# A Toeplitz block moved to VectorE, one load and one projection handed out earlier, in the convolution and scan stage of a hybrid encoder

## The chip, the cores and the metric

One NeuronCore of a Trainium2 chip runs the whole kernel. The metric is the device time of one execution in microseconds; lower is better. Engine names are those of the profile: PE is TensorE (PEld its weight loads), DVE is VectorE, ACT is ScalarE, POOL is GpSimd, SP is SyncE, whose queue here issues almost all DMAs.

## What is computed

The reference is a two-layer encoder on 512 positions and 1024 features. The change lies in the mixer of layer 0:

```python
z = h @ w_in                      # 1024 -> 512 (za) + 512 (zg) + 512 (u)
ya = conformer_conv(za, zg, ...)  # a = za * sigmoid(zg); depthwise conv of 31 taps
                                  # + conv_b; layer norm over channels; silu
yb = s5_mixer(u, ...)             # 32 groups of 16 channels, 64 complex states, two
                                  # directions; gelu; gated by sigmoid(y @ glu_w + glu_b)
x  = x + concat([ya, yb]) @ w_out
```

After it come a SwiGLU feed-forward, a layer of neighbourhood attention and a second feed-forward, which the change leaves alone.

## The kernel before, in words

**Scan.** The state-space branch is cut into chunks of 8 positions. Eight pieces of 4 groups go through the loop at lines 880 to 901. For piece `i`, PE makes the chunk inputs `v` (`piece_v`), ACT copies them to `vt`, and DVE runs the scan over chunks (`g_scan`, line 832: two multiplies, two scan instructions, a multiply and the sums into `S2`). In the same pass DVE prepares tables for piece `i+2` (`g_turn`) and `i+4` (`make_pb`), and PE transposes and multiplies pieces `i+2` (`piece_t`, `piece_k`). `piece_k` fills `kf`, the blocks of the response inside a chunk.

**Projections.** The matmuls for `zg` and `za` are a generator, `proj_all` (lines 723 to 752), which `heavy(n)` advances by n units. A unit is one 128x512 f32 matmul, which the trace shows as two records. There are 64: 32 for `zg`, then 32 for `za`. Each group of 8 takes one weight chunk from `W`. Of the last 8 units of `za`, every second one is followed by a DVE multiply at line 743, which gates one quarter of `an`. The loop calls `heavy(HV[0])` and `heavy(HV[1])`, with `HV = (3, 4)`: 7 units a pass, 56 in all. `heavy(100)` at line 928, after the loop, hands out the other 8. So on DVE the four gating multiplies stand behind the scan of piece 7.

**Weights.** While `W.hold` is set, `W.ahead()` after each chunk issues a load on SP into one of three `wraw` buffers. The load called at the last `za` chunk reuses the buffer of that same chunk, so it waits on SP until the last `za` matmul. After `heavy(100)`, loads come from `split()`, which also makes a high part (`whi`, ACT, line 89) and a low part (`wlo`, DVE, line 91).

**kd and T.** After the loop, four SP DMAs (lines 923 to 925) write `kf` to a DRAM buffer `kd`, and a POOL DMA (line 926) adds one more block to it. `T` (2 MB, lines 988 to 992) is read back from `kd` in the Toeplitz order. These three SP loads are issued after the convolution.

**Convolution.** `to_chunks(an, AC)` transposes the gated `an` on PE and copies it on ACT to `AC` (line 794). The convolution (lines 966 to 986) multiplies `AC` by Toeplitz blocks `tc`. They are made in pairs by `make_tc(n)`: 16 ACT instructions (line 765), each with one column of a mask as scale. There are three slots for pairs: two in `tca` and one in `tcb`. Pairs 0 and 2 are made in the scan loop, the others in the convolution: 4 ahead of it, and 6, 8, 10, 12, 14 after blocks 1, 3, 5, 7, 9. After every 4 blocks DVE adds `conv_b` (tile `cbB`, loaded by SP at line 954) and sums for the layer norm (lines 983 and 985).

**Order of DVE.** The tables `Q` for the scan's output (16 half tables of three DVE instructions each, `g_q`) are handed out by a planner, `bgV`. Each `tick(ns)` adds credit, each instruction takes its estimated cost from it, and `charge` takes credit for other DVE work. `W.ahead()` after block 7 puts two splits there (line 981).

**Output.** `out_y(i, hq)` multiplies `U` by `T` and `S2` by `Q`; `ln_mean()` follows the first `out_y` on PE, and DVE's subtraction at line 1053 follows it. `ln_scale()` with the matmul at line 1062 stands in the middle of the third `out_y`.

**Memory.** The pool `ep` ends at line 930, and the pool `lp` takes its place from the same address on: first `AC` (8704 bytes a partition), then four `Q` of 8192 bytes. `AC` so covers `vecs`, `work` and the scan's `vt`; `kf`, which lies 35424 bytes into `ep`, is covered by the last `Q`. A tile waits for the last use of what it covers.

```python
 22  HV = (3, 4)
882          heavy(HV[0])
888          heavy(HV[1])
891          run(g_scan(i))
926      PL.dma_start(out=kd_ap(7, 1), in_=kfr[0:16, 1], accum_op=ALU.add)
928      heavy(100)
977              if n % 2 and n + 5 < 16:
978                  make_tc(n + 5)
```

Of the kernel before, what the change touches and what calls it, by code (L numbers as in the profile page):

```python
# [9 lines left out]
F32 = mybir.dt.float32  # L10
# [3 lines left out]
ALU = mybir.AluOpType  # L14
# [4 lines left out]
QKV_ORDER = (0, 2, 1, 3, 4, 5)  # L19

CAP = 3000.0
HV = (3, 4)
QN, QT = 0, 2
LN, LT, LV = 1, 4, 6
LNA, MAH = (1, 3, 5), (0, 1, 2)
# [4 lines left out]
P = 128  # L30
# [4 lines left out]
G = 32  # L35
NCH = 64
LCH = 8
TAPS = 31
NLAG = 40
# [75 lines left out]
def tile_hybrid_encoder(ctx, tc, x, mix_norm, ffn_norm, ffn_w_gate, ffn_w_up, ffn_w_down,  # L115
# [4 lines left out]
    nc = tc.nc  # L120
    V, A, PE, PL = nc.vector, nc.scalar, nc.tensor, nc.gpsimd
# [41 lines left out]
    xp = ctx.enter_context(tc.tile_pool(name="xp", bufs=1))  # L163
# [17 lines left out]
    def xtile(name, dt=F32):  # L181

        i = xslot[0] % 10
        xslot[0] += 1
        if i < 8:
            return xp.tile([P, 512], dt, tag=f"x{i}", name=name)
        if i == 8:
            xpair_[:] = [xp.tile([P, 2, 512], dt, tag="x8", name=name)]
        return xpair_[0][:, i - 8]
# [83 lines left out]
    class Background:  # L273
# [20 lines left out]
        def tick(self, ns):  # L294
            self.credit = min(self.credit, CAP) + ns * self.share
            while self.credit > 0 and (self.jobs or self.fill):
                if self.jobs:
                    self.step()
                else:
                    self.step_fill()  # L300
# [31 lines left out]
    def pt(shape, name, pool=None, dt=F32):  # L332
        return (pool or mp).tile(shape, dt, tag=name, name=name)
# [78 lines left out]
    mask16 = pt([P, 16], "mask16")  # L412
# [24 lines left out]
    def tt(o, a, b, op):  # L437
        V.tensor_tensor(out=o, in0=a, in1=b, op=op)
        return cost(o.free_size())
# [180 lines left out]
    for k in range(KD):  # L620
        t = xtile("xT")
# [14 lines left out]
    def make_cb(i):  # L636
        cb = CB[i % 2]
        for d in range(2):
            h = slice(64 * d, 64 * d + 64)
            A.activation(out=cb[h, :, :, d], in_=CT[h, :, 4 * i:4 * i + 4], func=AF.Copy)  # L640
# [17 lines left out]
    for i in range(4):  # L658
# [7 lines left out]
        for kk in range(2):  # L666
            k = 2 * i + kk
            for j in range(4):
                c = slice(j * P, (j + 1) * P)
# [7 lines left out]
        if i == 1:  # L677
# [6 lines left out]
            for t in range(4):  # L684
# [4 lines left out]
                         in_=ps[:, 64:64 + 4 * TAPS].rearrange("p (t j) -> p t j", t=4), func=AF.Copy)  # L689
# [3 lines left out]
            for t in range(LCH):  # L693
                p0 = 64 * (t % 2) + 16 * (t // 2)
                nc.sync.dma_start(out=wv[p0:p0 + 16],
                                  in_=bass.AP(tensor=wdb.tensor, offset=wdb.offset + t,
                                              ap=[[WPAD, 16], [16 * WPAD, G], [1, NLAG]]))
            A.activation(out=hgb, in_=col[:, R_GB:R_GB + 4], func=AF.Copy, scale=0.5)
        if i == 2:
            for r in range(2):  # L700
                ps = psb("ct")
                for t in range(4):
                    PE.transpose(out=ps[:, t * P:(t + 1) * P],
                                 in_=cnat[r][:, t].rearrange("p d n -> p (d n)"), identity=ident)
# [50 lines left out]
    slots = [tca[:, 0], tca[:, 1]]  # L755
    wvs = wv.rearrange("p (h s) l -> p h s l", h=2)
    tcs = {}

    def g_tc(n):

        t = slots[n // 2 % 3]
        for i in range(2):
            tcs[n + i] = t[:, :, i]
        for c in range(16):
            A.activation(out=t[:, :, :, c], in_=wvs[:, :, n:n + 2], func=AF.Copy, scale=mask16[:, c:c + 1])
            yield 1

    def make_tc(n):
        for _ in g_tc(n):
            pass  # L770

    def g_tc_early():
        yield from g_tc(0)
# [2 lines left out]
    def heavy(n):  # L776
        for _ in range(n):
            if next(proj_all, 0) == 0:
                return
# [3 lines left out]
    def to_chunks(src, dst):  # L783

        tick(2000)
        for b in range(4):
            for t2 in range(2):
                h = slice(64 * t2, 64 * t2 + 64)
                ps = psb("U")
                for g in range(8):  # L790
                    PE.transpose(out=ps[0:64, g * 64:g * 64 + 64],
                                 in_=src[h, b * 8 + g].rearrange("p j c -> p (j c)"),
                                 identity=ident[h, h])
                A.activation(out=dst[h, b * 8:b * 8 + 8], in_=ps[0:64].rearrange("p (g k) -> p g k", g=8),
                             func=AF.Copy)
# [60 lines left out]
    def piece_v(i):  # L856

        g0 = 4 * i
        pp = ppb[:, i % 2]
        pv = psb("v")  # L860
        for q in range(2):
            for g in range(4):
                for c in range(0, P, VW):
                    PE.matmul(out=pv[c:c + VW, (q * 4 + g) * 64:(q * 4 + g + 1) * 64], lhsT=pp[:, q, g, c:c + VW],
                              rhs=U[:, g0 + g] if c == 0 else U[:, g0 + g, ::-1], start=True, stop=True)
        v = ep.tile([P, 2, 256], F32, tag="vt", name="vt", bufs=2)
        A.activation(out=v, in_=pv.rearrange("p (q n) -> p q n", q=2), func=AF.Copy)
        vin[i] = v
# [11 lines left out]
    for i in range(NPC):  # L880
        piece_v(i)
        heavy(HV[0])
        if i + 2 < NPC:
            piece_t(i + 2)
            piece_k(i + 2)
        if i + 4 < NPC:
            make_cb(i + 4)
        heavy(HV[1])
        if i + 1 < NPC:
# [12 lines left out]
    for h in range(2):  # L902
# [4 lines left out]
                     in1=dmask.unsqueeze(1).to_broadcast([P, G, 16]), op=ALU.mult)  # L907
# [7 lines left out]
    def kd_ap(slot0, nj, pairs=1, run=512):  # L915

        base = kd[:, :, :]
        return bass.AP(tensor=base.tensor, offset=base.offset + slot0 // 2 * 16 * 1024 + slot0 % 2 * 512,
                       ap=[[1024, 16 * nj]] + ([[16 * 1024, pairs]] if pairs > 1 else []) + [[1, run]])
# [4 lines left out]
    nc.sync.dma_start(out=kd_ap(8, 4), in_=kfr[64:128, 1])  # L924
    nc.sync.dma_start(out=kd_ap(9, 3), in_=kfr[16:64, 1])
    PL.dma_start(out=kd_ap(7, 1), in_=kfr[0:16, 1], accum_op=ALU.add)

    heavy(100)
    W.hold = False
    early.close()  # L930
    lp = mixp.enter_context(tc.tile_pool(name="lp", bufs=1))
    AC = pt([P, G, NCH + 4], "AC", lp)
    PL.memset(AC[:, :, 0:2], 0.0)
    PL.memset(AC[:, :, NCH + 2:NCH + 4], 0.0)

    Q = {i: lp.tile([P, 2, 8, 8, 16], F32, tag="Q", name="Q", bufs=4) for i in (0, 2, 1, 3)}

    def g_q(i, hf):
        g0 = 8 * i + 4 * hf
# [5 lines left out]
        for o, a, b, op in ((0, cr, ci, ALU.add), (1, ci, cr, ALU.subtract)):  # L945
            yield tt(w[0], wr, a, ALU.mult)
            yield tt(w[1], wi, b, ALU.mult)
            yield tt(Q[i][:, o, 4 * hf:4 * hf + 4], w[0], w[1], op)


    cbB = tmp([P, 16, 16], "rstdB", 1)
    for h in range(2):
        src = conv_b[0, 256 * h:256 * h + 256]
        nc.sync.dma_start(out=cbB[64 * h:64 * h + 64],
                          in_=bass.AP(tensor=src.tensor, offset=src.offset, ap=[[0, 64], [1, 256]]))
# [5 lines left out]
    tick(1000)  # L961
    to_chunks(an, AC[:, :, 2:NCH + 2])
    make_tc(4)
    yc = pt([P, LCH, 16, 16], "an")
    lns = tmp([P, 4, LCH], "lns", 1)
    for b in range(4):
        ps = psa("conv")
        for gi in range(4):
            n = 4 * b + gi
            t = tcs.pop(n)  # L970
            for h in range(2):
                for l in range(5):
                    PE.matmul(out=ps[64 * h:64 * h + 64, gi * P:gi * P + P],
                              lhsT=AC[:, 16 * h + n, l:l + NCH],
                              rhs=t[:, h, :, 8 * l:8 * l + 8],
                              start=(l == 0), stop=(l == 4))
            if n % 2 and n + 5 < 16:
                make_tc(n + 5)
            tick(2200)
        if b == 1:  # L980
            W.ahead()
        gs = slice(4 * b, 4 * b + 4)
        V.tensor_tensor(out=yc[:, :, gs], in0=ps.rearrange("p (g c t) -> p t g c", g=4, t=LCH),
                        in1=cbB[:, gs].unsqueeze(1).to_broadcast([P, LCH, 4, 16]), op=ALU.add)
        V.tensor_reduce(out=lns[:, b], in_=yc[:, :, gs].rearrange("p t g c -> p t (g c)"), axis=AX.X, op=ALU.add)
        bgV.charge(1200)

    T = xp.tile([P, LCH, G, 16], F32, tag="xgl", name="T")
    T2 = T.rearrange("p (m o) g c -> p m o (g c)", o=2)
    nc.sync.dma_start(out=T[0:64].rearrange("p (m o) g c -> p m (o g c)", o=2), in_=kd_ap(0, 4, 4, 1024))  # L990
    for o in range(2):
        nc.sync.dma_start(out=T2[64:128, :, o], in_=kd_ap(1 + o, 4, 4))

    yn = xp.tile([P, LCH, 16, 16], F32, tag="xgh", name="yn")

    def out_y(i, hq, between=None):
# [4 lines left out]
        for gi in range(4):  # L1001
            if gi == 2 and between is not None:
                between()
            for h in range(2):
                g = h * 16 + i * 8 + hq * 4 + gi
                o = ps[64 * h:64 * h + 64, gi * P:(gi + 1) * P]
                q8 = Q[g // 8]
                PE.matmul(out=o, lhsT=U[:, g], rhs=T[:, :, g], start=True, stop=False)
                for r in range(2):
# [6 lines left out]
    GC = 0.7978845608028654  # L1016
    yg = pt([P, 4, S], "AC", lp)

# [59 lines left out]
    def mix_tile(n):  # L1078
        return lp.tile([P, 4, S], F32R, tag="Q", name=n, bufs=4)

# [47 lines left out]
    for p2 in range(2):  # L1128
        wh, wl = W.next()
        W.ahead()  # L1130
        for mi in range(2):
            m = 2 * p2 + mi
            ps = psb("glu")
            for k in (0, 2, 1, 3):
                c = slice(mi * P, mi * P + P)
# [60 lines left out]
    for m in range(KD):  # L1196
        ps = psa("dn")
        for a, b in ((0, 8), (8, 16), (16, 22)):
            wh, wl = W.next()
            W.ahead()  # L1200
            for k in range(a, b):
                mm3(ps, wh[:, k - a], wl[:, k - a], gh[:, k], gl[:, k], k == 0, k == NF - 1)
        t = xtile("x2")
        V.tensor_tensor(out=t.rearrange("p (c t r) -> p t r c", **dims),
                        in0=ps.rearrange("p (t r c) -> p t r c", **dims),
                        in1=x1[m].rearrange("p (t r c) -> p t r c", **dims), op=ALU.add)
# [37 lines left out]
    def ring(name, dt=F32):  # L1244
        return ap_.tile([P, S], dt, tag="ring", name=name, bufs=6)
# [122 lines left out]
    for n, cg in enumerate(QKV_ORDER):  # L1368
# [46 lines left out]
        else:  # L1415
            ssh = tmp([P, 4, 8], "ssh")
            qs = []
            for j in range(4):
                t = ring("qs")
# [58 lines left out]
    for h in range(2):  # L1478
        for j in range(4):
# [4 lines left out]
            t = fp.tile([P, 512], F32, tag="xn3", name="xn3", bufs=4)  # L1484
# [3 lines left out]
        for i in range(NF // 2):  # L1488
# [5 lines left out]
            for kk, j in steps:  # L1494
                k = 2 * i + kk
                c = slice(j * P, (j + 1) * P)
# [4 lines left out]
        for j in range(4):  # L1501
            t = xn3[h, j]
# [30 lines left out]
```

## Time and profile before

| what | value |
|---|---|
| median of 3 runs | 1257.42 us (1256.78 to 1258.33) |
| profiled execution, its own time | 1258.42 us |
| span of its instructions | 1256.5 us |
| PE busy | 1213.6 us (97%) |
| DVE busy | 674.1 us (54%) |
| ACT busy | 470.1 us (37%) |
| POOL busy | 37.1 us (3%) |

The profile shows one execution. Its own time exceeds its span by 1.9 us, which lie around the instructions, and it lies 1.0 us above the median of the runs. Positions in the trace are us from the start of the span. In a timeline a row gives start, length, engine, line, operation, tile written and tiles read, count, and in brackets how long the engine was idle before and what ended that.

### The profile page before, as it was taken

The numbers are of one execution on the slowest core, as the hardware profiler recorded it, in microseconds if no ns is written. First come the engines' busy times: TensorE is split into PE (matmuls) and PEld (weight loads), VectorE is DVE, ScalarE is ACT, GpSimd is POOL, SyncE is SP. The second block draws the span as 40 slices with busy tenths as digits, with TensorE's granted clock in tenths as the row PEclk, the third lists the DMA queues.
The fourth block names the chain that finished last, engine by engine and source line by source line (L and its number), as shares of the span: only waits on it lengthen the run. The fifth ranks groups of instructions, "written<-read, shape, count | busy, mean of one in ns | idle before, by whom it ended". The sixth has DMA issues, their size and how long they took to land.

```text
span 1256.5 us, 16175 instructions
## 1 busy us (share of the span) xinstructions
PE 1213.6 (97%) x6427; PEld 961.7 (77%) x6427; DVE 674.1 (54%) x1163; ACT 470.1 (37%) x837; POOL 37.1 (3%) x90
## 2 busy tenths in 40 slices
PE   7999758999999999999999999999999999999998
PEld 3554557888888888888888887668888888888886
DVE  7999965764444444333337554655544444442322
ACT  4544575543333232222225455544333323231120
POOL 1000000000000000000000002320000000000000
PEclk9999898999999999999999999999999999999999
DMA  7411130333333333333343543212333333333321
GB/s 155 92 51 51 55 86 17 109 93 101 101 94 92 100 90 91 105 96 93 97 155 126 151 136 106 66 39 85 100 101 93 92 100 89 96 101 101 118 101 33
DMA packets 173154, 118.04 MB, mean 94 GB/s; under 512 B 21193, under 2 KB 153593, under 8 KB 173080
## 3 DMA queue, kind: packets, MB, share of 16 engines
q1 hardware_dynamic: 172616, 115.92, 31.9%
q10 hardware_dynamic: 400, 1.07, 0.4%
q8 instruction: 50, 0.82, 0.3%
q14 instruction: 24, 0.20, 0.1%
q0 software_dynamic: 64, 0.03, 0.0%
HBM read 109.04 MB, written 7.96 MB: 93 GB/s over the span
## 4 chain that ended last, share of the span: by engine, by line
PE 84%; ACT 3%; DMA 1%; DVE 1%; issue 0%; SPq 0%; POOL 0%; ACTq 0%; DVEq 0%; POOLq 0%
PE up L199 6%; PE gate L199 6%; PE gate L201 6%; PE up L201 6%; PE gate L200 6%; PE up L200 6%; PE qkv L1398 3%; PE qkv L1400 3%; PE qkv L1399 3%; PE dn L200 3%; PE dn L199 3%; PE dn L201 3%; PE dn L1499 3%; PE dn L1497 3%; PE dn L1498 3%; PE o L1360 3%
## 5 line engine op out<-in xcount | busy, mean ns | idle before, releaser
L91 DVE TENSOR_TENSOR wlo<-wraw,whi 128x1024 fp32r<-128x1024 f32 x176 | 212.9, 1213 | 265.7 <-ACT whi L89 264.4
L89 ACT ACTIVATE whi<-wraw 128x1024 fp32r<-128x1024 f32 x176 | 183.4, 1044 | 283.3 <-issue 113.9
L199 PE MATMUL gate<-xgh,whi 128*128 128x512 f32 x352 | 137.2, 390 | 0.0
L199 PE MATMUL up<-xgh,whi 128*128 128x512 f32 x352 | 137.1, 390 | 0.0
L201 PE MATMUL gate<-xgh,wlo 128*128 128x512 f32 x352 | 137.0, 389 | 0.0
L201 PE MATMUL up<-xgh,wlo 128*128 128x512 f32 x352 | 137.0, 389 | 0.0
L200 PE MATMUL gate<-xgl,whi 128*128 128x512 f32 x352 | 136.9, 389 | 0.0
L200 PE MATMUL up<-xgl,whi 128*128 128x512 f32 x352 | 136.9, 389 | 0.0
L1182 DVE TENSOR_TENSOR fu<-up,rstdB 128x512 f32<-128x512 f32 x44 | 30.4, 691 | 113.1 <-PE up L201 113.1
L1184 ACT ACTIVATE gh<-fu 128x512 fp32r<-128x512 f32 x44 | 27.8, 632 | 150.9 <-DVE fu L1183 150.9
L201 PEld LDWEIGHTS up<-xgh,wlo 128*128 128x128 f32 x352 | 66.1, 188 | 13.8
L201 PEld LDWEIGHTS gate<-xgh,wlo 128*128 128x128 f32 x352 | 66.0, 188 | 13.9
L199 PEld LDWEIGHTS gate<-xgh,whi 128*128 128x128 f32 x352 | 66.1, 188 | 13.7
L200 PEld LDWEIGHTS up<-xgl,whi 128*128 128x128 f32 x352 | 66.1, 188 | 13.7
L200 PEld LDWEIGHTS gate<-xgl,whi 128*128 128x128 f32 x352 | 66.1, 188 | 13.6
L199 PEld LDWEIGHTS up<-xgh,whi 128*128 128x128 f32 x352 | 66.0, 188 | 13.6
L199 PE MATMUL dn<-gh,whi 128*128 128x512 f32 x176 | 69.3, 394 | 0.0
L200 PE MATMUL dn<-gl,whi 128*128 128x512 f32 x176 | 69.3, 394 | 0.0
L201 PE MATMUL dn<-gh,wlo 128*128 128x512 f32 x176 | 69.3, 394 | 0.0
L1499 PE MATMUL dn<-whi,gl 128*128 128x512 f32 x176 | 69.2, 393 | 0.0
L1497 PE MATMUL dn<-whi,gh 128*128 128x512 f32 x176 | 69.0, 392 | 0.0
L1398 PE MATMUL qkv<-whi,xgh 128*128 128x512 f32 x176 | 68.8, 391 | 0.0
(293 smaller groups left out, 2052.8 us busy)
## 6 DMA issues: line engine op xcount, KB each, us to landing
wraw<-in_ffn_w_gate_dram SPq DMA_DIRECT2D x44, 512.0 KB
wraw<-in_ffn_w_up_dram SPq DMA_DIRECT2D x44, 512.0 KB
wraw<-in_ffn_w_down_dram SPq DMA_DIRECT2D x38, 512.0 KB
wraw<-in_na_w_qkv_dram SPq DMA_DIRECT2D x24, 512.0 KB
wraw<-in_ab_w_in_dram SPq DMA_DIRECT2D x12, 512.0 KB
bt<-bd SPq DMA_DIRECT2D x8, 640.0 KB
wraw<-in_ab_w_out_dram SPq DMA_DIRECT2D x8, 512.0 KB
wraw<-in_na_w_out_dram SPq DMA_DIRECT2D x8, 512.0 KB
```

The lines of the kernel that those rows point to most:

```text
L89: self.nc.scalar.activation(out=hi, in_=raw, func=AF.Copy)
L91: eng.tensor_tensor(out=lo, in0=raw, in1=hi.bitcast(F32), op=ALU.subtract)
L199: PE.matmul(out=o, lhsT=lh, rhs=rh, start=start, stop=False)
L200: PE.matmul(out=o, lhsT=lh, rhs=rl, start=False, stop=False)
L201: PE.matmul(out=o, lhsT=ll, rhs=rh, start=False, stop=stop)
L1360: PE.matmul(out=o[64 * e:64 * e + 64, j * P:(j + 1) * P], lhsT=vt[p0:p0 + n, kt, hc:hc + 64], rhs=pt_[p0:p0 + n, b, e], start=(b == 0), st ...
L1398: PE.matmul(out=pq[j], lhsT=lh, rhs=wh[:, kk], start=(k == 0), stop=False)
L1399: PE.matmul(out=pq[j], lhsT=lh, rhs=wl[:, kk], start=False, stop=False)
L1400: PE.matmul(out=pq[j], lhsT=ll, rhs=wh[:, kk], start=False, stop=(k == 7))
L1497: PE.matmul(out=pd[j], lhsT=gh[:, k, c], rhs=wh[:, kk], start=(k == 0), stop=False)
L1498: PE.matmul(out=pd[j], lhsT=gh[:, k, c], rhs=wl[:, kk], start=False, stop=False)
L1499: PE.matmul(out=pd[j], lhsT=gl[:, k, c], rhs=wh[:, kk], start=False, stop=(k == NF - 1))
```

## The change

- `HV` is (4, 4), so the 64 units of the two projections are all handed out inside the scan loop: the last 8, with their four gating multiplies and the weight load called among them, come in the pass of piece 7, before its scan and before the writes to `kd`. `heavy(100)` finds nothing left.
- The tile `T` and its three loads move from behind the convolution to right behind the writes to `kd`.
- `Q` is allocated before `AC` in the pool `lp`, so `AC` lies 32768 bytes into it.
- `make_tc(10)` makes its pair by four DVE `tensor_tensor` instructions of 128x640 instead of 16 ACT instructions of 128x160. The planner is not charged for them.

```diff
-HV = (3, 4)
+HV = (4, 4)
+TCV = 10
...
     def make_tc(n):
-        for _ in g_tc(n):
-            pass
+        if n != TCV:
+            for _ in g_tc(n):
+                pass
+            return
+        t = slots[n // 2 % 3]
+        for i in range(2):
+            tcs[n + i] = t[:, :, i]
+            for h in range(2):
+                V.tensor_tensor(out=t[:, h, i], in0=wvs[:, h, n + i].unsqueeze(1).to_broadcast([P, 16, NLAG]),
+                                in1=mask16.unsqueeze(2).to_broadcast([P, 16, NLAG]), op=ALU.mult)
...
     PL.dma_start(out=kd_ap(7, 1), in_=kfr[0:16, 1], accum_op=ALU.add)
+    T = xp.tile([P, LCH, G, 16], F32, tag="xgl", name="T")
+    T2 = T.rearrange("p (m o) g c -> p m o (g c)", o=2)
+    nc.sync.dma_start(out=T[0:64].rearrange("p (m o) g c -> p m (o g c)", o=2), in_=kd_ap(0, 4, 4, 1024))
+    for o in range(2):
+        nc.sync.dma_start(out=T2[64:128, :, o], in_=kd_ap(1 + o, 4, 4))
 
     heavy(100)
...
+
+    Q = {i: lp.tile([P, 2, 8, 8, 16], F32, tag="Q", name="Q", bufs=4) for i in (0, 2, 1, 3)}
     AC = pt([P, G, NCH + 4], "AC", lp)
     PL.memset(AC[:, :, 0:2], 0.0)
     PL.memset(AC[:, :, NCH + 2:NCH + 4], 0.0)
-
-    Q = {i: lp.tile([P, 2, 8, 8, 16], F32, tag="Q", name="Q", bufs=4) for i in (0, 2, 1, 3)}
...
-    T = xp.tile([P, LCH, G, 16], F32, tag="xgl", name="T")
-    T2 = T.rearrange("p (m o) g c -> p m o (g c)", o=2)
-    nc.sync.dma_start(out=T[0:64].rearrange("p (m o) g c -> p m (o g c)", o=2), in_=kd_ap(0, 4, 4, 1024))
-    for o in range(2):
-        nc.sync.dma_start(out=T2[64:128, :, o], in_=kd_ap(1 + o, 4, 4))
```

## Rows read from the trace of the kernel before

**Rows 1.** Page, busy tenths of PE in 40 slices of 31.4 us.

```profile
PE   7999758999999999999999999999999999999998
```

**Rows 2.** Timeline of PE around the scan's end, the convolution and the first output.

```profile
107.80 0.66 PE L632 MATMUL P<-ident,pb 128*128 128x128 f32 x4 [1.32 <-DVE pb L438]
109.86 0.66 PE L632 MATMUL P<-ident,pb 128*128 128x128 f32 x4 [1.40 <-DVE pb L438]
...
123.50 13.14 PE L734 MATMUL za<-wraw,xg 128*128 128x512 f32 x30
142.36 4.46 PE L791 MATMUL U<-ident,an 64*64 64x64 f32 x64 [5.72 <-DVE an L743]
...
146.74 6.29 PE L973 MATMUL conv<-tca,AC 128*64 128x128 f32 x80
...
158.87 3.44 PE L973 MATMUL conv<-tca,AC 128*64 128x128 f32 x40 [1.66 <-ACT tca L765]
...
181.16 4.04 PE L973 MATMUL conv<-tca,AC 128*64 128x128 f32 x34 [3.55 <-ACT tca L765]
...
192.71 0.66 PE L1008 MATMUL y<-T,U 128*64 128x128 f32 x2 [6.86 <-DMA T<-kd]
...
203.75 0.39 PE L1062 MATMUL var<-lnq,wpad 128*128 128x8 f32 x2 [0.30 <-ACT diag L1057]
```

**Rows 3.** Timeline of DVE over the same stretch.

```profile
133.87 1.23 DVE L438 TENSOR_TENSOR work<-phase,vt 128x1024 f32<-128x1024 f32 x1
...
139.82 2.48 DVE L743 TENSOR_TENSOR an<-an,za 128x512 f32<-128x512 f32 x4
142.22 1.28 DVE L438 TENSOR_TENSOR sq<-pwQ,CT 128x512 f32<-128x512 f32 x2
...
156.53 0.68 DVE L983 TENSOR_TENSOR an<-conv,rstdB 128x512 f32<-128x512 f32 x1
...
157.85 1.28 DVE L438 TENSOR_TENSOR sq<-pwQ,CT 128x512 f32<-128x512 f32 x2
...
175.09 2.36 DVE L91 TENSOR_TENSOR wlo<-wraw,whi 128x1024 fp32r<-128x1024 f32 x2 [9.07 <-ACT whi L89]
...
199.14 2.35 DVE L1053 TENSOR_TENSOR an<-an,mean 128x1024 f32<-128x1024 f32 x2 [7.71 <-PE mean L1049]
```

**Rows 4.** Timeline of ACT in the convolution.

```profile
143.58 4.91 ACT L794 ACTIVATE AC<-U 64x512 f32<-64x512 f32 x8 [10.28 <-DVE sq L438]
...
163.82 5.19 ACT L765 ACTIVATE tcb<-wv,mask 128x160 f32<-128x160 f32 x16
...
174.02 1.99 ACT L89 ACTIVATE whi<-wraw 128x1024 fp32r<-128x1024 f32 x2
```

**Rows 5.** Timeline of the SP queue, end of the scan.

```profile
121.66 8.51 SPq L72 DMA_DIRECT2D wraw<-in_ab_w_out_dram  x2
130.22 1.15 SPq L923 DMA_DIRECT2D kd<-kf  x2
...
132.05 0.59 SPq L925 DMA_DIRECT2D kd<-kf  x1
136.67 0.38 SPq L72 DMA_DIRECT2D wraw<-in_ssm_glu_w_dram  x1
```

**Rows 6.** POOL's timeline, the added block; and its landing (DMA issues: KB, us).

```profile
134.78 0.84 POOL L926 DMA_DIRECT2D kd<-kf  x1 [21.14 <-DMA kd<-kf]
...
kd<-kf POOLq DMA_DIRECT2D x1, 32.0 KB, 2.4
```

**Rows 7.** Chain of waits, 133 to 200 us: the load of T.

```profile
180.22 12.41 DMA T<-kd
```

**Rows 8.** Stretches: length, busy time (records) of each engine, granted PE clock, DMA share, GB/s.

```profile
142.36:146.74 4.38, 4.38 (x64) 4.29 (x64) 4.19 (x7) 3.04 (x6) 0.00 (x0) 0.55 0.01 4
...
192.70:198.10 5.40, 5.39 (x49) 5.23 (x49) 0.00 (x0) 0.00 (x0) 0.00 (x0) 0.55 0.00 0
198.10:203.50 5.40, 5.36 (x81) 5.09 (x80) 2.35 (x2) 3.70 (x16) 0.00 (x0) 1.00 0.02 5
```

## The prediction

> **What bounds the kernel now.** I read the busy tenths first: PE is full but for the first slice and slices 4 to 6, 126 to 220 us [rows 1]. So a gain can only come from that stretch, and I read it engine by engine. PE's timeline shows whom it waits for: 5.72 us for the gated `an`, then in the convolution 1.66 us a pair for ACT's Toeplitz blocks (3.55 us for the last), then 6.86 us for `T` [rows 2]. ACT makes a pair in 5.19 us where PE uses one in 3.44 [rows 2, 4]. The chain of waits says the same: ACT through the convolution, then the DMA of `T`, 12.41 us from its last issue [rows 7]. DVE's timeline is to be read with it: DVE works without a gap until 166.0, waits 9.07 us for `whi`, and works again until 191.43, where its next idle of 7.71 us begins [rows 3]. So DVE ends its work before the layer-norm mean only 1.2 us ahead of the output matmuls at 192.71. That is the next limit, and the sum has to be made along DVE.
>
> **Part 1, HV.** The last 8 `za` units end at 123.50 + 13.14 = 136.64. PE does the same work in another order. Each pass gets one unit more (13.14 / 15 = 0.88 us), so PE reaches the transposes of piece 7 about six units, 5.3 us, later, and the waits of 1.32 and 1.40 us there for DVE's `pb` vanish [rows 2]. `za` ends at 136.64 - 2.72 = 133.92. The later `v` matmuls cost nothing, because ACT's copy of `v` stands behind scan tables that DVE itself sets free; without that cover DVE would start a scan late by what is missing. On DVE the scan of piece 7 runs from 133.87 to 139.82 and the gating to 142.22 [rows 3]. With the two exchanged, gating starts at about 133.9 and ends at 136.3, and the scan still ends at 142.22. So DVE gains nothing here; `an` is ready 6.0 us sooner.
>
> **The queue that part 1 moves.** The load called at unit 57 now stands on SP ahead of the writes to `kd`. It waits for the last `za` matmul (at 136.67 before, 0.03 after `za`), and everything behind it on SP waits too. The load ahead of `kd` now ended its issue at 130.17; from its start, 0.38 earlier, the writes, the added block at 134.78 and its landing 2.4 later took 7.4 us [rows 5, 6]. Starting from 133.95 they end at 141.35. In the new place, 32768 to 41472 bytes into the pool, `AC` covers `kf` (35424 on), so it can be written only from about 141.4. ACT's copies to `AC` begin there instead of 143.58 [rows 4]: 2.2 us are gained, not 6.0. Without the exchange of `Q` and `AC` they would wait for `work`, thus for the scan's end.
>
> **Part 2, block 10 on DVE.** ACT loses 5.19 us [rows 4]. DVE gets four instructions of 128x640. Its `Q` multiplies, which read inputs broadcast the same way, take 1.28 us for two of 128x512 [rows 3]; by size that is 0.80 each, 3.2 in all. Bounds: 2.4 (0.6 each, no more than 128x512 takes when overlapped) and 6.4 (twice the row); I take 3.2, from the nearest row. By the planner's credit they come one `Q` instruction after the first bias addition, at about 158.5, when the pair that used the slot before has long been multiplied.
>
> **Part 3, T early.** SP can issue the three loads from 141.4, in some 1.9 us. Counted from the last issue as before [rows 7], `T` lands at about 155.7. Who needs it is past 177, so the wait of 6.86 us goes. Behind them on SP stands only the bias `cbB`, needed by DVE at 156.5.
>
> **The sum along ACT.** The copies to `AC` are 2.2 us earlier and a pair is gone: `whi` begins at 174.02 - 7.4 = 166.6, and `wlo` could begin 1.07 us after that, at 167.7 [rows 3, 4]. The last pair is ready at 181.16 - 7.4 = 173.8, multiplied by 177.2, and the first output, 5.4 us at worst [rows 8], ends by 182.6.
>
> **The sum along DVE.** `Q` from 142.22; first bias addition at 156.53, `Q` again at 157.85, until 166.02 (175.09 - 9.07) [rows 3]; plus 3.2 is 169.2. By then `whi` has been there for 1.5 us, so the idle of 9.07 us is gone. From `wlo` to the last layer-norm sum took 191.43 - 175.09 = 16.34 us [rows 3]: 185.6. This is after PE's 182.6, so DVE ends last, and PE waits for it. The mean matmul takes some 1.1 us (198.05 to 199.14), so DVE's subtraction starts at 186.7 instead of 199.14: **12.4 us earlier**.
>
> **What is given back.** PE idles some 3 to 5 us before the mean. [...] Between mean and the variance matmul at 203.75 PE has 4.35 us of output matmuls at full clock (199.1 to 203.45) [rows 2]. If the clock is low for 4.9 us from 185.7, 3.9 of them fall on these and do 2.1 us of work; the rest ends at 192.7, where the variance is due at 203.75 - 12.4 = 191.3. This costs 1.4 us; bounds 0 (clock not lowered) and 3.5 (low throughout). What follows is PE and short DVE and ACT steps in the same order, then PE alone, and shifts as a whole.
>
> **Total: -12.4 + 1.4 = -11.0 us**, against the profiled execution 1258.42 - 11.0 = 1247.4. That execution lies 1.0 above the median of the runs shown, 1257.42, so the median to expect is **1246.4**.
>
> **Rivals.**
> - *The writes to `kd` come later than 141.4.* For it: three queues in a row (SP, POOL, a landing), shown once only. Against it: the weight load in front is of the same size in both orders. Up to 1.5 us of delay cost nothing; beyond that `whi` delays `wlo` one for one. If `AC` starts as late as before, 143.58, this is 0.7 us; if 3 to 4 us later still, 1250 to 1251.
> - *The clock is low through all of the output matmuls, or not at all*: 1248.5 or 1245.
> - *`cbB` behind 2 MB of `T` makes it slower.* Place: DVE's first bias addition at 156.5, with all of DVE behind it. Before, `cbB` had the queue to itself. With `T` landing at 155.7 and 128 KB more behind it, `cbB` lands at 156 to 157, a tie. Each us past 156.5 costs one: at 168 all of the gain is gone, from 170 on the kernel is slower by over 0.2%. For that `T` would need twice the 12.41 us [rows 7], which were measured with weight loads on the same engines. Time 1247 at a tie, 1260 at double. [...] No row here shows two such loads one behind the other with the second needed first.
> - *The change doesn't do what it says*: the wait for `T` turns into one of the same length for DVE. This is partly in the sum already. If `Q` slowed while `T` is written, or the four instructions cost 6.4 us or more, 1250; if DVE also waited for `za` or `v`, by some 8 us, no change.
>
> **How the numbers follow.** The sum as worked out has 0.68. Late `kd` writes have 0.12, the clock at either end 0.10, `cbB` late 0.06 (half of it slower, the rest between), the change without effect 0.04. About 0.2%, 2.5 us, is what a measurement of this kernel can tell from no change. Faster by more holds in the first three and part of the others: 0.92; within it 0.04; slower 0.04. The range goes down to 1243.9 (no loss to the clock, the four instructions at 2.4 us, and the spread of the runs below the median, 0.6) and up to 1250.5, which takes in `kd` writes late by some 5 us, or the instructions at 6.4 us; what lies outside has less than 0.2.
>
> **What would show it.** `za` ends near 134 and gating stands before the last scan on DVE; `AC` copies begin near 141.4 with POOL's added block just before them; no idle of DVE before `wlo`; `T` lands near 156, no wait on it; PE waits 3 to 5 us before the mean, ended by DVE; the subtraction at line 1053 starts near 186.7. It is wrong if DVE waits anywhere between 134 and 185, for `cbB`, `whi` or `an`, or if the mean doesn't wait for DVE.

## The result, and the profile after

The changed kernel takes **1246.11 us** (median of 4 runs, 1245.8 to 1246.4) against 1257.43 us before (4 runs). The ratio is 0.9909 with a 95% interval of 0.9892 to 0.9927: it is faster by 11.3 us, and 1246.4 was forecast. The profiled execution takes 1246.06 us against 1258.42.

Where the time went is read at a few points of the stage. The third column is the prediction's. The changed execution is past the scan of piece 6 already 0.8 us earlier (133.08 against 133.87), before anything in the sum begins, and that much of each difference isn't the change's: 0.7 us of it is there at the first multiply of the scan of piece 0 (58.70 against 59.37). There the executions with the old `HV` shown below begin at 58.55 (`t_and_tc`) and 58.83 (`undo_hv`), so it isn't `HV` either.

| point (us from the start) | before | predicted | after |
|---|---|---|---|
| last `za` matmul ends | 136.64 | 133.9 | 132.65 |
| gating of `an` ends | 142.30 | 136.3 | 135.56 |
| first ACT copy to `AC` | 143.58 | 141.4 | 141.62 |
| `whi` begins | 174.02 | 166.6 | 166.98 |
| `wlo` begins | 175.09 | 169.2 | 168.10 |
| last convolution pair begins | 181.16 | 173.8 | 174.12 |
| last layer-norm sum ends | 191.43 | 185.6 | 184.44 |
| subtraction at the mean begins | 199.14 | 186.7 | 185.12 |
| variance matmul | 203.75 | 192.7 | 191.76 |

DVE's timeline after. Lines below 766 of the source have moved by one, those in the convolution and behind it by 9 to 14: the bias addition is L997, the sum L999, the subtraction L1062.

```profile
133.08 2.48 DVE L744 TENSOR_TENSOR an<-an,za 128x512 f32<-128x512 f32 x4
135.48 1.22 DVE L439 TENSOR_TENSOR work<-phase,vt 128x1024 f32<-128x1024 f32 x1
...
141.42 1.29 DVE L439 TENSOR_TENSOR sq<-pwQ,CT 128x512 f32<-128x512 f32 x2
...
155.74 0.68 DVE L997 TENSOR_TENSOR an<-conv,rstdB 128x512 f32<-128x512 f32 x1
...
157.66 3.03 DVE L778 TENSOR_TENSOR tcb<-wv,mask 128x640 f32<-128x640 f32 x4
...
168.10 2.35 DVE L92 TENSOR_TENSOR wlo<-wraw,whi 128x1024 fp32r<-128x1024 f32 x2
...
183.75 0.69 DVE L999 TENSOR_REDUCE lns<-an 128x8 f32<-128x512 f32 x1
185.12 2.35 DVE L1062 TENSOR_TENSOR an<-an,mean 128x1024 f32<-128x1024 f32 x2 [0.69 <-PE mean L1058]
192.19 0.17 DVE L219 TENSOR_SCALAR rs_a<-var 128x8 f32<-128x8 f32 x1 [4.71 <-PE var L1071]
```

Against [rows 3]: gating stands ahead of the last scan, and from there to 184.44 no row has a bracket, that is, DVE never waits. The 9.07 us before `wlo` and the 7.71 us before the subtraction are gone; 0.69 us is left. What DVE got is the row at 157.66.

PE's timeline after.

```profile
125.52 7.13 PE L735 MATMUL za<-wraw,xg 128*128 128x512 f32 x16
135.62 2.36 PE L800 MATMUL U<-ident,an 64*64 64x64 f32 x32 [2.96 <-DVE an L744]
142.27 2.91 PE L800 MATMUL U<-ident,an 64*64 64x64 f32 x32 [4.29 <-ACT AC L803]
...
174.12 3.11 PE L987 MATMUL conv<-tca,AC 128*64 128x128 f32 x37 [2.96 <-ACT tca L766]
...
184.49 0.60 PE L1058 MATMUL mean<-lns,wpad 128*128 128x8 f32 x2 [3.54 <-DVE lns L999]
...
191.76 0.39 PE L1071 MATMUL var<-lnq,wpad 128*128 128x8 f32 x2
```

Against [rows 2]: PE starts the transposes 6.7 us sooner, then stands before ACT's copies (4.29 us). No row waits for `T`; the wait before the mean names DVE's last sum, as the sum along DVE said.

SP and POOL after: the weight load now stands ahead of the writes to `kd`, and `T` follows the added block.

```profile
132.69 0.37 SPq L73 DMA_DIRECT2D wraw<-in_ssm_glu_w_dram  x1
133.11 1.15 SPq L932 DMA_DIRECT2D kd<-kf  x2
...
139.72 0.62 SPq L938 DMA_DIRECT2D T<-kd  x1
...
137.33 0.84 POOL L935 DMA_DIRECT2D kd<-kf  x1 [22.42 <-DMA kd<-kf]
141.67 0.16 POOL L949 MEMSET AC<- 128x64 f32 x1 [3.50 <-DVE S L439]
```

The clock and the DMA in stretches after (columns as in [rows 8]).

```profile
150.00:152.00 2.00, 2.00 (x32) 2.00 (x30) 1.93 (x4) 2.00 (x8) 0.00 (x0) 1.00 0.67 135
152.00:154.00 2.00, 2.00 (x31) 2.00 (x30) 1.93 (x4) 2.00 (x8) 0.00 (x0) 1.00 0.00 0
...
175.00:178.00 3.00, 3.00 (x49) 3.00 (x48) 2.90 (x6) 0.00 (x0) 0.00 (x0) 1.00 0.00 0
...
187.00:190.00 3.00, 3.00 (x32) 3.00 (x31) 0.48 (x1) 2.68 (x14) 0.00 (x0) 0.51 0.02 5
```

The transfer of `T`, and of `cbB`, issued behind it, is over by 152. PE works at half clock (granted 0.50 to 0.52) from the mean to about 190. The squares that the variance sums end on ACT at 189.69:

```profile
189.50 0.19 ACT L1066 ACTIVATION_READ_ACCUMULATOR diag<-an 128x1 f32 x1
```

### The profile page after: what moved, and what is told of

It reads as the page before. It is cut to its first block, busy times and chain, and to the rows that moved or that the text cites. A ratio compares the mean times of both kernels' runs of the same rounds, so it can differ in the third digit from the quotient of the medians.

```text
span 1244.0 us, 16159 instructions
## 1 busy us (share of the span) xinstructions
PE 1211.6 (97%) x6427; PEld 961.6 (77%) x6427; DVE 675.9 (54%) x1167; ACT 465.5 (37%) x821; POOL 37.4 (3%) x90
## 4 chain that ended last, share of the span: by engine, by line
PE 85%; DVE 3%; issue 0%; POOL 0%; DVEq 0%; POOLq 0%
PE up L200 6%; PE gate L200 6%; PE gate L202 6%; PE up L201 6%; PE gate L201 6%; PE up L202 6%; PE qkv L1407 4%; PE qkv L1409 4%; PE qkv L1408 4%; PE dn L200 3%; PE dn L202 3%; PE dn L201 3%; PE dn L1508 3%; PE dn L1506 3%; PE dn L1507 3%; PE o L1369 3%
```

## The experiments

Theory 1 is the forecast's: DVE, busy without a gap from the last scan to the last layer-norm sum, sets the time of the mean, and ACT's chain runs just below it. The rivals: the gain is the sum of the single waits taken from PE; ACT alone or DVE alone sets the time; the place of `AC` matters. Every edit is against the changed kernel unless it says otherwise.

### Only one part undone: the projections

```diff
-HV = (4, 4)
+HV = (3, 4)
```

> HV back to (3, 4), all else as in the changed kernel. Theory 1 (DVE is busy without a gap from the last scan to the last layer-norm sum and sets the time of the mean; ACT's convolution chain runs just below it): DVE has the same work in another order, ACT's first copy to AC comes after the gating, near 142.7 instead of 141.6, whi 1.1 us later than 167.0, so wlo waits about 1 us: 1247.1 us (1246.5 to 1247.8). Rival 2 (the gain is the sum of the single waits that were taken from PE): the 6 us by which the gated an is ready sooner come back: about 1252.

Measured: 1246.07 us, ratio 0.9909 (0.9896 to 0.9923). The same as the changed kernel, and just below what was expected (1246.5 to 1247.8); the rival's 6 us don't come back. DVE's timeline shows both the wait that was expected and why it isn't seen in the time.

```profile
169.49 2.36 DVE L92 TENSOR_TENSOR wlo<-wraw,whi 128x1024 fp32r<-128x1024 f32 x2 [1.04 <-ACT whi L90]
...
186.32 2.35 DVE L1062 TENSOR_TENSOR an<-an,mean 128x1024 f32<-128x1024 f32 x2 [0.48 <-PE mean L1058]
192.65 0.17 DVE L219 TENSOR_SCALAR rs_a<-var 128x8 f32<-128x8 f32 x1 [3.98 <-PE var L1071]
```

The subtraction is 1.2 us later than after the change (185.12), the step behind the variance only 0.46 (192.19): PE idles 1.9 instead of 3.5 us before the mean, and its granted clock is 0.97 from 184 to 187 and 0.50 from 187 to 190, where the changed kernel has 0.50 and 0.51; so part of the delay is absorbed in PE's work up to the variance.

### Only one part undone: block 10

```diff
-TCV = 10
+TCV = -1
```

> Block 10 made on ACT again, all else as in the changed kernel. Theory 1 (DVE line): ACT's chain is 5.2 us longer, DVE's 3.0 us shorter; whi near 172.2, DVE idle before wlo about 8 us, wlo near 173.3 instead of 168.1, the mean near 189.6 instead of 184.5: 1251.2 us (1250.3 to 1252). Rival 3 (DVE was the end of the chain with room on ACT, so the instructions only burden DVE): 3 us faster, 1243.

Measured: 1250.7 us, ratio 0.9946 (0.9934 to 0.9958), 4.6 us slower than the changed kernel, within the forecast; the rival with 1243 falls.

```profile
173.39 2.36 DVE L92 TENSOR_TENSOR wlo<-wraw,whi 128x1024 fp32r<-128x1024 f32 x2 [7.90 <-ACT whi L90]
...
190.22 2.35 DVE L1062 TENSOR_TENSOR an<-an,mean 128x1024 f32<-128x1024 f32 x2 [0.48 <-PE mean L1058]
```

The wait for `whi` is back (7.90 us, forecast about 8), and the subtraction moves with `wlo`, by 5.1 and 5.3 us.

### Only one part undone: T

The tile and its load are taken from behind the writes to `kd` and put behind the convolution again:

```diff
...
-    T = xp.tile([P, LCH, G, 16], F32, tag="xgl", name="T")
...
@@ behind the convolution @@
+    T = xp.tile([P, LCH, G, 16], F32, tag="xgl", name="T")
...
```

> T loaded behind the convolution again, all else as in the changed kernel. Theory 1 (DVE line): the loads are issued near 171.5 on SP, T lands near 185, past the time at which DVE ends (184.4); the first output follows at the low clock, the mean near 190.5 instead of 184.5, of which some 1.5 us come back since PE then reaches the variance at full clock: 1250.7 us (1249.5 to 1252.5). Rival 2 (sum of PE's single waits): the whole wait between the convolution's end (177.5) and the landing, 8 us: 1254. Rival 4 (the transfer is hidden behind DVE anyway): 1246.

Measured: 1251.09 us, ratio 0.9947 (0.9934 to 0.9961), 5.0 us slower than the changed kernel, as theory 1 has it. Neither is the transfer hidden behind DVE, nor does the whole wait count. PE's timeline, and the chain of waits:

```profile
187.99 0.66 PE L1018 MATMUL y<-T,U 128*64 128x128 f32 x2 [7.67 <-DMA T<-kd]
192.95 1.06 PE L1059 MATMUL mean<-lns,wpad 128*128 128x8 f32 x8
198.65 0.39 PE L1072 MATMUL var<-lnq,wpad 128*128 128x8 f32 x2 [0.30 <-ACT diag L1067]
```

```profile
174.39 13.51 DMA T<-kd
```

This execution is the slowest of the five (1252.67). PE waits 7.67 us for `T`, whose transfer stands on the chain from 174.39 to 187.90. The variance comes 4.6 us after the subtraction here (194.04 to 198.65) and 6.6 us after it in the changed kernel (185.12 to 191.76), which gives 2.0 us back.

### Only one part undone: the place of AC

```diff
     lp = mixp.enter_context(tc.tile_pool(name="lp", bufs=1))
-    Q = {i: lp.tile([P, 2, 8, 8, 16], F32, tag="Q", name="Q", bufs=4) for i in (0, 2, 1, 3)}
     AC = pt([P, G, NCH + 4], "AC", lp)
...
+    Q = {i: lp.tile([P, 2, 8, 8, 16], F32, tag="Q", name="Q", bufs=4) for i in (0, 2, 1, 3)}
```

> AC allocated ahead of Q again, so that it covers the scan's work and vt; all else as in the changed kernel. Theory 5 (AC waits for the release of the whole pool that it replaces, wherever it lies): no change, ACT's first copy to AC within 0.2 us of 141.6, right after the scan's last sum: 1246.1 us (within 0.5). Rival 6 (AC waits only for what it covers, thus for kf when behind Q and for the scan when in front): the copies would not be bound by the scan in the changed kernel; with AC in front they come later, by up to 1.7 us, and the time rises by up to 1.5 us.

Measured: 1246.46 us, ratio 0.9914 (0.9900 to 0.9927), not to be told from the changed kernel. ACT's timeline:

```profile
142.05 4.91 ACT L803 ACTIVATE AC<-U 64x512 f32<-64x512 f32 x8 [9.05 <-DVE S L439]
```

The first copy is 0.43 us later than after the change (142.05 against 141.62), and so is DVE's own work in this execution: its first bias addition begins at 156.16 instead of 155.74. The copies follow the scan's last sum, `S`, in both. In the built program the instruction stream of ACT waits, ahead of the first copy, for DVE's count at the scan's end, for the writes to `kd` and for the added block, wherever `AC` lies: the new pool waits for the whole pool that it replaces. `undo_hv`, where `AC` lies behind `Q` too, shows it apart from the added block. There the block has landed by 136.55, when the first load of `T` goes out, but POOL's first write to `AC` begins 0.3 us after the scan's last sum (139.27):

```profile
139.56 0.16 POOL L949 MEMSET AC<- 128x64 f32 x1 [4.55 <-DVE S L439]
```

### T and block 10 alone

```diff
-HV = (4, 4)
+HV = (3, 4)
...
```

`AC` is also allocated ahead of `Q`, by the edit of the section before.

> Only T early and block 10 on DVE; HV back to (3, 4) and AC ahead of Q as in the kernel before. Theory 1 (DVE's line sets the mean; handing out za sooner and the place of AC change neither DVE's work nor the wait for the scan's end): 1246.2 us (1245.6 to 1247.2). Rival 6 (the place of AC and the earlier gating matter together): 1248 or more.

Measured: 1246.0 us, ratio 0.9905 (0.9889 to 0.9922). The two edits are the whole change; the other two are worth nothing that can be measured, singly or together.

### More work for DVE

```diff
-        if n != TCV:
+        if n not in (10, 12):
```

> Blocks 10 and 12 both made on DVE (8 instructions of 128x640 instead of 4), all else as in the changed kernel. Theory 1 (DVE is busy without a gap up to the mean): 3.0 us more on DVE, ACT's further relief of 5.2 us is worth nothing; mean near 187.4: 1249.0 us (1248.2 to 1249.8). Rival 7 (ACT's chain of blocks still sets the time): faster, down to 1243.

Measured: 1249.09 us, ratio 0.9934 (0.9922 to 0.9947); its runs (1248.23 to 1249.62) lie 3 us above those of the changed kernel (1245.8 to 1246.4). ACT was relieved by another block and that bought nothing. DVE's and PE's timelines:

```profile
166.20 3.02 DVE L778 TENSOR_TENSOR tca<-wv,mask 128x640 f32<-128x640 f32 x4
...
188.09 2.35 DVE L1062 TENSOR_TENSOR an<-an,mean 128x1024 f32<-128x1024 f32 x2 [0.69 <-PE mean L1058]
```

```profile
187.46 0.59 PE L1058 MATMUL mean<-lns,wpad 128*128 128x8 f32 x2 [4.71 <-DVE lns L999]
```

3.02 us put on DVE move the subtraction by 2.97.

### Less work for DVE, through POOL

```diff
-                V.tensor_tensor(out=t[:, h, i], in0=wvs[:, h, n + i].unsqueeze(1).to_broadcast([P, 16, NLAG]),
+                PL.tensor_tensor(out=t[:, h, i], in0=wvs[:, h, n + i].unsqueeze(1).to_broadcast([P, 16, NLAG]),
```

> Block 10 made by four POOL instructions instead of four DVE instructions, all else as in the changed kernel. Theory 1 (DVE line): DVE's line is 3.0 us shorter, but ACT's whi at 167.0 then holds wlo at 168.0 instead of 168.1 (DVE is free at 165.0), so nearly nothing: 1246.0 us (1245.3 to 1246.5), with an idle of DVE of about 3 us before wlo. Rival 8 (DVE alone sets the time, with room on ACT): 3 us faster, 1243. Should POOL need more than 8 us for the four, convolution pair 10 is late and the time rises.

Measured: 1246.3 us, ratio 0.9913 (0.9899 to 0.9926). The time is as theory 1 said, but not for its reason: DVE has no idle before `wlo` (168.26). The timelines of POOL and DVE:

```profile
153.41 6.64 POOL L778 TENSOR_TENSOR tcb<-wv,mask 128x640 f32<-128x640 f32 x4 [11.33 <-PE conv L987]
```

```profile
153.97 3.30 DVE L439 TENSOR_TENSOR sq<-pwQ,CT 128x512 f32<-128x512 f32 x2
157.30 1.63 DVE L439 TENSOR_TENSOR Q<-sq 128x512 f32<-128x512 f32 x1
158.86 0.68 DVE L997 TENSOR_TENSOR an<-conv,rstdB 128x512 f32<-128x512 f32 x1
```

While POOL works, DVE's `Q` instructions take 3.30 and 1.63 us instead of 1.29 and 0.69. The 2.95 us that this costs are about what the move had saved (3.03). So this run doesn't decide between theory 1 and rival 8: DVE's work didn't get shorter.

The two `wlo` of the convolution, numbers 12 and 13 of the splits, made on POOL:

```diff
     W.charge = bgV.charge
+    W.on_pool = (12, 13)
```

> The two wlo that stand in the convolution made on POOL, the planner not charged for them, all else as in the changed kernel. Theory 1 (DVE line): DVE loses 2.3 us and no longer waits for whi there; the mean comes 2.3 us sooner, near 182.2, still later than the last convolution pair (177.5) and the first output (180.1): 1243.8 us, and up to 1 us less because PE idles less ahead of the mean. Rival 7 (ACT or PE sets the time of the mean): 1246.

Measured: 1246.61 us, ratio 0.9915 (0.9901 to 0.9928): nothing gained where 2.3 us were forecast. The timelines of POOL and DVE:

```profile
168.20 5.13 POOL L92 TENSOR_TENSOR wlo<-wraw,whi 128x1024 fp32r<-128x1024 f32 x2 [26.18 <-ACT whi L90]
```

```profile
169.51 4.36 DVE L440 TENSOR_TENSOR sq<-pwQ,CT 128x512 f32<-128x512 f32 x2
```

Two `Q` instructions take 4.36 us, 3.07 more than alone: DVE loses more than the 2.35 us of the two `wlo`. So this run doesn't speak against theory 1; it shows that such work, moved to POOL, isn't off DVE.

### PE's order around the mean

```diff
-    ln_mean()
     out_y(0, 1)
+    ln_mean()
```

> The second output group stands ahead of the mean on PE instead of behind it, all else as in the changed kernel. Theory 9 (PE's idle of 3.5 us before the mean, and the low clock after it, make the variance 2.1 us late): the group fits into that idle, DVE's subtraction still starts near 185.1, the variance comes when the squares are done, near 189.8 instead of 191.8: 1244.2 us (1243.8 to 1245). Rival 10 (what follows the mean is bound by the DVE and ACT steps, the low clock costs nothing): 1246.

Measured: 1246.92 us (1245.62 to 1249.32), ratio 0.9919 (0.9905 to 0.9932). No gain, and not a clean test. The timelines of POOL and PE:

```profile
140.09 0.84 POOL L935 DMA_DIRECT2D kd<-kf  x1 [22.80 <-DMA kd<-kf]
142.87 0.16 POOL L949 MEMSET AC<- 128x64 f32 x1 [1.93 <-DVE sq L439]
```

```profile
175.39 5.78 PE L987 MATMUL conv<-tca,AC 128*64 128x128 f32 x37 [2.96 <-ACT tca L766]
...
186.83 1.06 PE L1058 MATMUL mean<-lns,wpad 128*128 128x8 f32 x8
192.53 0.39 PE L1071 MATMUL var<-lnq,wpad 128*128 128x8 f32 x2 [2.92 <-ACT diag L1066]
```

In this execution the last `za` matmul ended 2.4 us later (135.08) and the added block was issued 2.8 us later, so that the copies to `AC` began at 142.90, and the last pair ran at a granted clock of 0.50. PE reached the mean at 186.83, behind DVE's last sum (185.7). The second group made the mean late instead of filling an idle. The variance then waits for the squares, as theory 9 has it. Whether the low clock's cost can be had back this way stays open.

### Two edits to go on from

The last six `Q` instructions of DVE put behind the mean:

```diff
-            tick(2200)
+            if n < 12:
+                tick(2200)
```

> The changed kernel with no planner tick for blocks 12 to 15, so that the last six Q instructions of DVE come behind the mean's subtraction instead of ahead of the last layer-norm sum. Theory 1 (DVE's line sets the mean, and DVE idles 4.7 us after the subtraction): the last sum ends near 180.3 instead of 184.4, the subtraction starts near 181.1 instead of 185.1, and the six fit into the idle; PE no longer idles before the mean and stays at the high clock, so the variance comes 6 us sooner: 1240.3 us (1239.5 to 1242.5). Rival 7 (ACT and PE set the time of the mean) or rival 11 (what follows the mean is as long as DVE's idle): 1245 to 1246.

Measured: **1242.88 us**, ratio 0.9878 (0.9863 to 0.9892), 3.2 us faster than the changed kernel, but 2.6 us above the forecast and outside its range (1239.5 to 1242.5). The timelines of PE and DVE:

```profile
180.49 1.06 PE L1059 MATMUL mean<-lns,wpad 128*128 128x8 f32 x8
186.21 0.39 PE L1072 MATMUL var<-lnq,wpad 128*128 128x8 f32 x2 [0.30 <-ACT diag L1067]
191.87 1.79 PE L1085 MATMUL cT<-ident,an 64*128 64x64 f32 x29 [0.92 <-DVE an L1078]
```

```profile
181.59 2.35 DVE L1063 TENSOR_TENSOR an<-an,mean 128x1024 f32<-128x1024 f32 x2 [0.79 <-PE mean L1059]
...
187.23 0.69 DVE L439 TENSOR_TENSOR Q<-sq 128x512 f32<-128x512 f32 x1
187.84 0.16 DVE L219 TENSOR_SCALAR rs_a<-var 128x8 f32<-128x8 f32 x1
```

Theory 1 holds: the subtraction is 3.5 us sooner, PE doesn't idle before the mean, and the variance comes 5.6 us sooner. The forecast missed what follows: the six end at 187.84, behind the variance's end (186.6), so 1.2 us of the saving are lost, and PE then waits 0.92 us for DVE. That is rival 11 in part.

Pair 4 made ahead of the copies to `AC`, alone and with the edit before:

```diff
-    to_chunks(an, AC[:, :, 2:NCH + 2])
     make_tc(4)
+    to_chunks(an, AC[:, :, 2:NCH + 2])
```

> The changed kernel with block pair 4 made on ACT ahead of the copies to AC, in the 9 us in which ACT waits for the scan's end. Theory 1: ACT's chain is 3 to 5 us shorter, the last convolution pair starts near 171 instead of 174.1, but DVE's line is as before: 1246.0 us (1245.2 to 1246.4). Rival 7 (ACT sets the end): 1242 to 1243.

Measured: 1245.49 us, ratio 0.9900 (0.9886 to 0.9915).

> Both edits together: no planner tick for blocks 12 to 15, and pair 4 ahead of the copies to AC. Theory 1: as without the second edit, DVE's last sum near 180.3, now with more room on ACT and PE: 1240.0 us (1239 to 1242). Rival 7: 3 us below the first edit alone.

Measured: **1241.38 us**, ratio 0.9870 (0.9855 to 0.9885). ACT's timeline with both edits:

```profile
132.44 5.21 ACT L766 ACTIVATE tcb<-wv,mask 128x160 f32<-128x160 f32 x16
141.34 4.92 ACT L803 ACTIVATE AC<-U 64x512 f32<-64x512 f32 x8 [3.69 <-DVE S L439]
149.72 10.64 ACT L766 ACTIVATE tca<-wv,mask 128x160 f32<-128x160 f32 x33 [3.46 <-PE conv L987]
```

The pair fits into ACT's wait, but ACT then stands 3.46 us for PE to free a slot, and alone it gains 0.6 us, which is not told from nothing. In that run `whi` begins 1.7 us sooner (165.31), but the subtraction at the mean stays where it was (185.14 against 185.12): DVE sets the time. The version with both is the fastest, 16.5 us below the kernel before and 4.7 below the changed one (runs of 1240.56 to 1243.55 against 1245.8 to 1246.4). Its lead of 1.5 us over the first edit alone lies within what the two intervals overlap, and half of the 3 us that rival 7 asked for. The two profiled executions differ by 0.76 us, of which 0.63 is there already in the scan of piece 0 (58.44 against 59.07); so nearly nothing of it is the second edit's.

## Why the prediction was right

**The bound.** "So DVE ends its work before the layer-norm mean only 1.2 us ahead of the output matmuls at 192.71": making the sum along DVE for this reason carried the forecast. A sum of PE's waits (5.72 for `an`, 6.86 for `T`, some 5 of the convolution) would have given 17.6 us. Three us more on DVE make the kernel 3 us slower although ACT has a block less, 4.0 us of DVE work put behind the mean make it 3.2 us faster, and a pair taken out of ACT's chain into its idle moves the subtraction by 0.02 us. The 1.2 us themselves are not the room that counts. DVE's last sum lay 6.6 us ahead of the mean matmul (191.43 against 198.05), and with `T` early but block 10 on ACT the time falls by 6.8 us (1257.46 to 1250.7).

**Part 2 and part 3.** The four instructions were taken at 3.2 us and took 3.03. Undone singly, block 10 costs 4.6 us and `T` 5.0, which is 9.6, and together they are the whole 11.3. The single costs don't add up, because the mean waits for the later of two lines: with block 10 undone it is DVE's, whose last sum ends at 189.74, and with `T` undone it is PE's, which begins the mean at 192.95.

**Part 1 was mis-sized.** I gave it 2.2 us on ACT's chain, with 1.5 us of slack for DVE's `wlo`, which makes 0.7 us of the time. The runs give 0 (1246.07 and 1246.0). On DVE it is neutral, as said; the 1.1 us that ACT gains by it is the wait of 1.04 us before `wlo` when it is undone, and the lag behind the mean swallows most of that.

**The place of AC was read wrongly.** "Without the exchange of `Q` and `AC` they would wait for `work`, thus for the scan's end": they wait for `work`, and for `kf`, in either place, since the whole pool is released at once, and not, as was said of the memory, tile by tile. That the number came out (141.4 against 141.62) is luck. The added block landed at 139.6 (137.33 and 2.3 to landing), not at 141.35, and what ended last was the scan's last sum, at 141.39; by the prediction's own rows that was due at 142.2. In the executions of `y_first` and `undo_t`, two of the eleven profiled with `HV` at (4, 4), `kd` was later and the landing ended last; the copies began at 142.90 and 143.13. So the rival with the late writes to `kd` is real.

**The clock.** Taken at 1.4 us with bounds 0 and 3.5; measured 2.1: the squares are done at 189.69 and the variance starts at 191.76. The 4.9 us, and 2.1 us of work in 3.9, were an estimate from the first two stretches of [rows 8], which stand behind longer idles [rows 2]; no run had shown them for the idle before the mean. The low stretch, granted 0.50 to 0.52, is as long as taken (185.0 to 190, against 4.9), but nearly all of it falls on output matmuls, where I had counted 3.9, since most of the mean matmul was done before the last sum arrived.

**The rival on the other side, `cbB` behind T,** had 3.7 us to spare. I took 12.41 us from the last issue, a row with a megabyte of weights on the same engines; without them the transfer is over by 152, and DVE's bias addition at 155.74 follows `Q` without a wait. The chance of 0.06 took for granted that `cbB` lands behind `T`; whether it did or passed it, no row shows.

**The total.** The subtraction came 14.0 us sooner, 12.4 forecast; 0.8 of the difference is the earlier start, 0.4 the mean matmul, most of which was done before the last sum arrived. The lag of the variance took 2.0 back where 1.4 was forecast, which leaves 12.0 us at the variance (203.75 to 191.76). Without the earlier start that is 11.2, and the medians give 11.3. So that the sum's 11.0 comes so close is partly luck: without the earlier start the subtraction came 0.8 us sooner than forecast, and the lag was 0.6 larger.

## What to carry to other kernels

When several engines run a stage with little slack between them, add up each engine's own line from one common point to the step where they meet; the time moves only with the last one, and a wait taken away is worth no more than the distance to the next line. After such a change look at what the bounding engine does ahead of the meeting point that nobody needs yet: here six table instructions, moved by one condition, gave another 3 us. Allocation order inside a pool that replaces another isn't a lever if the whole old pool is released at once: look at what the waiting instruction really waits for.

## What the runs showed of the hardware

Beside POOL's work some instructions of DVE took longer. In `pool_tc` POOL ran four instructions of 1.64 to 1.71 us from 153.41 to 160.05; meanwhile two `sq` multiplies of DVE begun at 153.97 took 3.30 us instead of 1.29, and the `Q` instruction at 157.30 took 1.63 instead of 0.69. In `pool_wlo` POOL ran its two `wlo` from 168.20 to 173.33, and the two multiplies begun at 169.51 took 4.36 us. But the bias additions, which read one input from PSUM, took their usual 0.68 us beside POOL, at 158.86 in `pool_tc` and at 168.19 in `pool_wlo`, and so did the sums behind them (0.69). What makes the difference is not shown.

The same idle of PE was followed by different clocks. Before the last convolution pair PE idled 2.96 us both in the changed kernel and in `pool_wlo`. Behind it the granted clock was 1.00 (175 to 178) in the one, and in the other 0.52:

```profile
175.00:178.00 3.00, 3.00 (x25) 3.00 (x24) 2.91 (x5) 0.00 (x0) 0.00 (x0) 0.52 0.42 147
```

The pair took 3.4 us in the changed kernel and 5.0 in `pool_wlo`. As DVE ended later in both, this did not reach the mean; in `y_first` it did. What made the difference is not shown.
